# Diagonal 2-D prefix sum: the last 16 rows of the last batch loaded in batch 0 by ScalarE's DMA queue

## The chip, the cores and the metric

One core of one Trainium2 chip runs the kernel. The metric is the device time of one execution in microseconds (us). Before the change the median of three runs is 667.26 us (667.2 to 668.1).

## The reference

The input `x` is 4 batches of 4224 x 4224 fp32 numbers. The output is, per batch, the running sum along the diagonal of the two-dimensional prefix sum:

```python
ps = np.cumsum(np.cumsum(x, axis=1), axis=2)
diag = np.diagonal(ps, axis1=1, axis2=2)
return np.cumsum(diag, axis=1).astype(np.float32)
```

Every element of a batch is needed: element (i, j) enters all diagonal sums from max(i, j) on. So the kernel has to read 4 x 4224 x 4224 x 4 bytes, 285.5 MB, and to write 67.6 KB.

## The kernel before

**The main stream.** A batch is read in strips of 768 rows (`F2 * P`, six rows on each of 128 partitions) and one of 384 rows. GpSimd issues these loads (`load_rows`, L74 to L78), and the DMA turns fp32 into bf16 on the way. Three strip buffers are used in turn, so a load is issued as soon as the strip that lay in its buffer three strips earlier has been summed. Of a strip, `add_up` (L349 to L379) sums what lies left of the diagonal block by rows (ScalarE, `act_sum`, L258, and VectorE, `row_sums`, L267) and what lies right of it by columns (TensorE matmuls with a column of ones). The diagonal block is split by a triangular mask on VectorE. When a batch is through, matmuls put the row sums into groups, and two scans make the prefix sums.

**The last batch** is cut so that little work is left behind its last byte. Its last 384 rows do not come as one strip. A first piece, columns 3696 on of rows 3840 to 4095, was loaded at the very start by SyncE's queue as fp32 (`head`, L68). The rest of these 256 rows comes in two pieces (`part_a`, L451). The last 128 rows, columns 0 to 4095, come in four blocks of `R` = 32 rows (`part_b`, L462). A row of a block is cut in four pieces of 1024 columns, so that a block fills 128 partitions; its sums then go through `weights4`, a matrix that says how often the row on partition p counts for output i when four partitions hold one row. The last block is loaded in two DMAs, columns 0 to 767 of each piece and the other 256 (`bcut`, L453).

**The tail's order of work** is written out by hand (L528 to L581). Blocks 0 to 3 of `part_b` are summed as they come: block 0 by TensorE, block 1 and block 2 each in one ScalarE and one VectorE instruction (`act_sum`, `pair_sum`), block 3 in one ScalarE and two VectorE instructions (L571 to L573). An addition on VectorE (L557) stands between block 2 and block 3. Three matmuls (L579) bring the sums of block 3 into `fin_e`, VectorE copies that out (L580), and SyncE's queue stores the last 32 outputs (L581).

**Queues.** GpSimd's DMA queue (the page's q0, software_dynamic) carries all the bf16 loads in the order of issue. SyncE's (q1, hardware_dynamic) carries `head` and the outputs. ScalarE issues no DMA. The instructions of the engines are fetched through queues of their own (q8 and q14).

Of the kernel before, what the change touches and what calls it, by code (L numbers as in the profile page):

```python
# [8 lines left out]
FP32 = mybir.dt.float32  # L9
BF16 = mybir.dt.bfloat16  # L10
I32 = mybir.dt.int32
AX = mybir.AxisListType
ALU = mybir.AluOpType
# [4 lines left out]
def kernel(  # L18
# [14 lines left out]
    nc = tc.nc  # L33

    B, H, W = x.shape
    N = H
    P = 128
# [4 lines left out]
    LB = B - 1  # L42
    LG = NG - 1
    T0 = LG * GW
    TB = N - P
# [3 lines left out]
    consts = ctx.enter_context(tc.tile_pool(name="consts", bufs=1))  # L49
# [4 lines left out]
    last = ctx.enter_context(tc.tile_pool(name="last", bufs=1))  # L54
# [13 lines left out]
    head = last.tile([P, 2, HC], FP32, name="head")  # L68
    nc.sync.dma_start(out=head, in_=src_a[:, :, N - HC : N])

    def strip_tile():
        return strips.tile([P, F2, N], BF16, name="strip")

    def load_rows(o, b, r0):  # L74
        f = o.shape[1]
        nc.gpsimd.dma_start(  # L76
            out=o, in_=x[b, r0 : r0 + f * P, :].rearrange("(p f) w -> p f w", f=f)
        )  # L78
# [20 lines left out]
    def upper_mask(f):  # L99
# [22 lines left out]
        out=um1,  # L122
        in_=um1,
        compare_op=ALU.is_gt,
        fill=0.0,
        base=0,
        pattern=[[1, GW]],
        channel_multiplier=-1,
# [5 lines left out]
        out=ident,  # L134
        in_=ident,
        compare_op=ALU.is_equal,
        fill=0.0,
        base=0,
        pattern=[[-1, P]],
        channel_multiplier=1,  # L140
# [27 lines left out]
    def between_groups(name, turned):  # L168
# [27 lines left out]
        out=weights,  # L196
        in_=weights,
        compare_op=ALU.is_ge,
        fill=0.0,
        base=0,  # L200
        pattern=[[1, GW]],
        channel_multiplier=-1,
# [3 lines left out]
    R = P // 4  # L206
# [3 lines left out]
        out=steps, in_=steps, scalar=2, op=ALU.arith_shift_right  # L210
    )
    weights4 = consts.tile([P, P], FP32, name="weights4")
    nc.vector.tensor_scalar_max(out=weights4, in0=steps, scalar1=0.0)

    ident_h = consts.tile([P, P], BF16, name="ident_h")
    nc.vector.tensor_copy(out=ident_h, in_=ident)

    def matmul(o, lhsT, rhs, start=False):
        nc.tensor.matmul(  # L219
            o, lhsT=lhsT, rhs=rhs, start=start, stop=False, skip_group_check=True  # L220
        )
# [36 lines left out]
    def act_sum(acc, src, own=None):  # L258
        w = src.shape[-1]
        dump = own  # L260
        if dump is None:
            dump = dumpool.tile([P, 2176], BF16, name="dump")
        nc.scalar.activation(  # L263
            out=dump[:, :w], in_=src, func=ACT.Copy, accum_out=acc
        )

    def row_sums(acc, src):  # L267
        nc.vector.reduce_sum(out=acc, in_=src, axis=AX.X)  # L268
# [3 lines left out]
    def pair_sum(acc, src):  # L272

        w = src.shape[-1] // 2
        pair = last.tile([P, w], FP32, name=f"pair{len(pairs)}")
        pairs.append(pair)
        nc.vector.scalar_tensor_tensor(
            out=pair[:, :w],
            in0=src[:, :w],
            scalar=1.0,  # L280
            in1=src[:, w:],
            op0=ALU.mult,
            op1=ALU.add,
            accum_out=acc,
        )
# [32 lines left out]
        masked(hmu[:, h, :w], head[:, h, HC - w : HC], um1[:, :w], hu[:, h : h + 1])  # L318
    nc.vector.tensor_sub(out=asum[:, :, 0], in0=hs[:, 0:2], in1=hu[:, 0:2])

    whole_sums = last.tile([NG, LB, GW], FP32, name="whole_sums")
    last_sums = last.tile([NG, GW], FP32, name="last_sums")

    for b in range(B):
# [10 lines left out]
        def row_of(j):  # L335
            return (j + t0) % NG
# [12 lines left out]
        def add_up(strip, f, r0, acc, um, wp=0, ws=None, by_rows=False):  # L349


            nw = f * P // GW
            g = r0 // GW
            hi = r0 + f * P
            for j in range(g + nw + by_rows, NG):
                for q in range(f):
                    columns(j, 0, GW, strip[:, q, j * GW : (j + 1) * GW], q > 0)
            if ws is None:
                ws = scalar_cols(r0)
            mu = mup.tile([P, f, f * P], BF16, name=f"mu{f}")  # L360
            block = strip[:, :, r0:hi]
            nc.vector.tensor_mul(out=mu, in0=block, in1=um)  # L362
            nc.vector.tensor_sub(out=block, in0=block, in1=mu)  # L363
            if by_rows:
                rowed = mup.tile([P, GW], FP32, name="rowed")
                row_sums(
                    rowed,
                    strip[:, :, hi : hi + GW].rearrange("p q c -> p c q"),
                )
            for h in range(nw):  # L370
                for q in range(f):
                    columns(g + h, 0, GW, mu[:, q, h * GW : (h + 1) * GW], q > 0)
            if by_rows:
                k = row_of(g + nw)
                matmul(d, sel_f[:, NG - 1 - k : 2 * NG - 1 - k], rowed)
            for q in range(f):
                if ws > wp:
                    act_sum(acc[:, q, 0:1], strip[:, q, wp:ws])
            row_sums(acc[:, :, 1], strip[:, :, ws:hi])  # L379
# [12 lines left out]
        for s in range(ns):  # L392
            strip = prefetched.pop(0) if prefetched else None
            if strip is None:
                strip = strip_tile()
                load_rows(strip, b, s * F2 * P)
            add_up(
                strip, F2, s * F2 * P, acc6[:, s], um6, by_rows=whole and s > 0
            )
            if not whole and s == 0:  # L400
                diag_b = last.tile([P, P], BF16, name="diag_b")
                nc.gpsimd.dma_start(out=diag_b, in_=x[b, TB:N, TB:N])
            if not whole and s == 1:
                row_sums(hs[:, 2:3], diag_b)
                masked(hmu[:, 2, :P], diag_b, um1[:, :P], hu[:, 2:3])
                nc.vector.tensor_sub(out=dtot, in0=hs[:, 2:3], in1=hu[:, 2:3])
                for h in range(3):
                    columns(LG, h * P, GW, hmu[:, h, : GW - h * P], h > 0)
        a6 = acc6[:, :ns]
        sum_up(a6)  # L410
        for h in range(2):
            ps = slice(h * HP, (h + 1) * HP)
            k = row_of(h)
            nc.vector.tensor_copy(  # L414
                out=r6[ps, k : k + 2 * ns : 2, :], in_=a6[ps, :, :, 1]
# [27 lines left out]
        if not whole:  # L443

            strip = strip_tile()
            part_a = strip[:, 0:2]
            part_b = strip[:, 2, :TB].rearrange("p (s c) -> p s c", s=4)
            spare = strip[:, 3, :]
            acuts = [(1536, N - HC), (0, 1536)]
            for c0, c1 in acuts:  # L450
                nc.gpsimd.dma_start(out=part_a[:, :, c0:c1], in_=src_a[:, :, c0:c1])  # L451
            CB = TB // 4
            bcut = 768  # L453
            for sb, c0, c1 in (
                (0, 0, CB),
                (1, 0, CB),
                (2, 0, CB),
                (3, 0, bcut),
                (3, bcut, CB),
            ):  # L460
                r0 = TB + sb * R
                nc.gpsimd.dma_start(  # L462
                    out=part_b[:, sb, c0:c1],
                    in_=x[b, r0 : r0 + R, :TB].rearrange("r (k c) -> r k c", k=4)[
                        :, :, c0:c1
                    ],
                )

            fold_a = psum_s.tile([P, 2, 256], FP32, name="fold_a")
            c0, c1 = acuts[0]  # L470
            fcuts = [c0, c0 + 768, c0 + 2048, c1]
# [13 lines left out]
        c1 = mup.tile([NG, GW], FP32, name="c1")  # L485
# [10 lines left out]
        for i, (to, src) in enumerate(((c1, d), (c2, c1))):  # L496
            nc.vector.tensor_tensor_scan(  # L497
                out=to,
# [14 lines left out]
        fin_e = psum_s.tile([1, R], FP32, name="fin_e")  # L513
# [7 lines left out]
        def weigh_b(rows, w, r0=0, start=False):  # L521

            m = P - R - r0
            matmul(fin_b[:, r0:], rows, w[..., :m], start=start)
            matmul(fin_e, rows, w[..., m : m + R], start=start)


        c0, c1 = acuts[1]  # L528
# [5 lines left out]
        nc.scalar.copy(out=by, in_=by_ps)  # L534
        weigh_b(dtot, weights, start=True)
        weigh_b(ones_col[0:1], last_sums[0:1, M0:])


        row_sums(asum[:, :, 1], fold_a)
# [10 lines left out]
        esum = last.tile([P, 3], FP32, name="esum")  # L550
        act_sum(bsum[:, 0, 0:1], part_b[:, 1, :512], spare[:, :512])
        pair_sum(bsum[:, 0, 1:2], part_b[:, 1, 512:])
        for i in (1, 0):
# [5 lines left out]
            out=out[:LB, :].rearrange("b (g i) -> g b i", i=GW), in_=whole_sums  # L559
        )  # L560
        nc.sync.dma_start(
            out=out[b, :T0].rearrange("(g i) -> g i", i=GW), in_=last_sums[1:NG]
        )
        nc.sync.dma_start(
            out=out[b, T0 : T0 + M0].unsqueeze(0), in_=yl[:, :M0]
        )
        for i in (1, 0):
            weigh_b(bsum[:, 1, i : i + 1], weights4, 2 * R)


        act_sum(esum[:, 0:1], part_b[:, 3, :320], spare[:, 960:1280])  # L571
        pair_sum(esum[:, 1:2], part_b[:, 3, 320:bcut])
        pair_sum(esum[:, 2:3], part_b[:, 3, bcut:])  # L573
        nc.scalar.copy(out=yl[:, M0:E0], in_=fin_b)
        nc.sync.dma_start(
            out=out[b, T0 + M0 : T0 + E0].unsqueeze(0), in_=yl[:, M0:E0]
        )
        for k in (1, 0, 2):
            matmul(fin_e, esum[:, k : k + 1], weights4[:, :R])  # L579
        nc.vector.tensor_copy(out=ye, in_=fin_e)  # L580
        nc.sync.dma_start(out=out[b, T0 + E0 : N].unsqueeze(0), in_=ye)  # L581

# [29 lines left out]
```

## Time and profile before

| | |
|---|---|
| median of 3 runs | 667.26 us (667.2 to 668.1) |
| span of the profiled execution, first to last instruction | 665.7 us (the page gives no other time of it) |
| VectorE busy | 379.8 us (57%) |
| TensorE busy | 214.2 us (32%) |
| ScalarE busy | 135.3 us (20%) |
| GpSimd busy | 31.7 us (5%) |
| read from memory over the span | 285.47 MB, 429 GB/s |
| last data needed, seen by the waiting instruction | between 662.62 and 662.96 us |

The DMA lines of the page count the bytes as they are written, that is bf16 for the loads through GpSimd's queue: a packet of 25344 bytes there has read 50688. The share of an engine's busy time is a mean over stages; what holds the time is read from who waits for whom.

### The profile page before, as it was taken

To read this page: it belongs to the slowest core of one execution; us is meant where nothing else is said; L and a number is where in the kernel's file an instruction comes from. 1 tells how busy PE (TensorE), PEld (TensorE's weight loads), DVE (VectorE), ACT (ScalarE), POOL (GpSimd) and SP (SyncE) were. 2 spreads that over 40 slices of the span, in tenths; PEclk is the share of its full clock that TensorE was granted. 3 is DMA by queue.
4 is the path that set the end of the run, shared out by engine and by line. 5 is a ranking of instruction groups with operands and counts; after the bars stand their busy time and mean duration, and the time that the engine had idled before them with its cause. 6 is when DMAs were issued, how large, how long until landed. Compare 5 with 4: busy or idle time off the path is not lost.

```text
span 665.7 us, 2592 instructions
## 1 busy us (share of the span) xinstructions
PE 214.2 (32%) x998; PEld 98.5 (15%) x998; DVE 379.8 (57%) x176; ACT 135.3 (20%) x219; POOL 31.7 (5%) x60
## 2 busy tenths in 40 slices
PE   0070522302118143140311623403031253250468
PEld 0030211100003021010100311201000121120224
DVE  4160928476946173756793526466589443352766
ACT  0000121406300103040630020304063002030433
POOL 4200000000000000000000000000000000001000
PEclk9995856566558585765555958567555595765779
DMA  9999999999999999999999999999999999999998
GB/s 203 219 218 219 219 219 219 209 212 216 219 221 216 218 220 217 219 216 210 216 218 218 219 216 218 219 218 219 216 212 216 221 218 215 218 218 219 215 206 163
DMA packets 7667, 143.25 MB, mean 215 GB/s; under 512 B 698, under 2 KB 998, under 8 KB 2150
## 3 DMA queue, kind: packets, MB, share of 16 engines
q0 software_dynamic: 7312, 142.47, 99.9%
q1 hardware_dynamic: 342, 0.61, 0.3%
q8 instruction: 8, 0.13, 0.1%
q14 instruction: 5, 0.04, 0.0%
HBM read 285.47 MB, written 0.07 MB: 429 GB/s over the span
## 4 chain that ended last, share of the span: by engine, by line
DVE 51%; another core or an unknown queue 35%; DMA 12%; PE 1%; issue 1%; POOL 1%; DVEq 0%; POOLq 0%
DVE acc L268 27%; DMA strip<-in_x_dram 12%; DVE mu L362 7%; DVE strip L363 7%; DVE rowed L268 7%; PE d L219 1%; DVE c L497 0%; DVE whole_sums L497 0%; POOL strip L462 0%; DVE pu L268 0%; DVE whole_sums L288 0%; POOL strip L451 0%; DVE acc L387 0%; DVE rows L414 0%
## 5 line engine op out<-in xcount | busy, mean ns | idle before, releaser
L263 ACT ACTIVATE dump<-strip 128x416 bf16<-128x416 bf16 (+5 forms) x105 | 122.0, 1161 | 519.4 <-DMA strip<-in_x_dram 516.7
L362 DVE TENSOR_TENSOR mu<-strip,um 128x4608 bf16<-128x4608 bf16 (+1 forms) x24 | 52.4, 2183 | 256.9 <-DMA strip<-in_x_dram 256.7
L268 DVE TENSOR_REDUCE acc<-strip 128x6 f32<-128x4608 bf16 (+6 forms) x23 | 195.9, 8518 | 0.4
L226 PEld LDWEIGHTS <-sel 128*11 128x11 bf16 x643 | 66.7, 104 | 474.8 <-issue 445.4
L219 PE MATMUL d<-strip,sel 128*11 128x384 bf16 x90 | 37.3, 415 | 279.9 <-DMA strip<-in_x_dram 279.9
L226 PE MATMUL d<-strip,sel 128*11 128x384 bf16 x441 | 117.1, 409 | 13.8 <-DMA strip<-in_x_dram 13.8
L363 DVE TENSOR_TENSOR strip<-strip,mu 128x4608 bf16<-128x4608 bf16 (+1 forms) x24 | 52.4, 2183 | 1.0
L219 PE MATMUL d<-mu,sel 128*11 128x384 bf16 x43 | 16.0, 373 | 108.4 <-DVE mu L362 108.4
L268 DVE TENSOR_REDUCE rowed<-strip 128x384 f32<-128x2304 bf16 x12 | 48.9, 4076 | 0.0
L226 PE MATMUL d<-mu,sel 128*11 128x384 bf16 x200 | 45.7, 363 | 0.0
L76 POOL DMA_DIRECT2D strip<-in_x_dram x23 | 15.7, 683 | 537.2 <-DVE acc L268 291.8
L263 ACT ACTIVATION_READ_ACCUMULATOR dump<-strip 128x1 f32 x105 | 19.5, 186 | 0.0
L219 PE MATMUL d<-rowed,sel_f 128*11 128x384 f32 x24 | 11.7, 573 | 21.7 <-DVE rowed L268 21.7
L219 PEld LDWEIGHTS <-sel 128*11 128x11 bf16 x134 | 13.7, 102 | 24.8 <-issue 12.7
L219 PE MATMUL d<-ident,rows 128*11 128x128 f32 x24 | 5.2, 378 | 16.8 <-DVE rows L423 16.8
L219 PE MATMUL fold<-um,ident_h 128*128 128x512 bf16 x28 | 7.9, 454 | 0.0
L268 DVE TENSOR_REDUCE pu<-d 11x1 f32<-11x384 f32 x4 | 2.2, 546 | 6.2 <-PE d L219 6.2
L102 DVE MEMSET um<- 128x4608 bf16 (+1 forms) x2 | 4.9, 2458 | 1.1 <-issue 1.1
L103 POOL TENSOR_SCALAR_AFFINE_SELECT um<-um 128x4608 bf16<-128x4608 bf16 (+1 forms) x2 | 5.2, 2612 | 7.2 <-DVE um L102 7.2
L219 PEld LDWEIGHTS d<-rowed,sel_f 128*11 128x11 f32 x24 | 1.4, 92 | 26.4 <-DVE rowed L268 26.1
L219 PEld LDWEIGHTS d<-ident,rows 128*11 128x11 f32 x24 | 2.6, 118 | 18.5 <-DVE rows L423 11.7
L219 PE MATMUL d<-halves,rows 128*11 128x64 f32 x48 | 5.3, 289 | 0.0
(119 smaller groups left out, 75.0 us busy)
## 6 DMA issues: line engine op xcount, KB each, us to landing
strip<-in_x_dram POOLq DMA_DIRECT2D x18, 6336.0 KB, 72.7
strip<-in_x_dram POOLq DMA_DIRECT2D x7, 3168.0 KB, 55.7
strip<-in_x_dram POOLq DMA_DIRECT2D x1, 1080.0 KB, 49.9
strip<-in_x_dram POOLq DMA_DIRECT2D x1, 768.0 KB, 52.9
strip<-in_x_dram POOLq DMA_DIRECT2D x3, 256.0 KB, 54.1
head<-in_x_dram SPq DMA_DIRECT2D x1, 528.0 KB, 3.9
strip<-in_x_dram POOLq DMA_DIRECT2D x1, 192.0 KB, 43.2
strip<-in_x_dram POOLq DMA_DIRECT2D x1, 64.0 KB, 28.6
```

The costliest lines, as they stand in the source:

```text
L76: nc.gpsimd.dma_start(out=o, in_=x[b, r0 : r0 + f * P, :].rearrange("(p f) w -> p f w", f=f))
L102: nc.vector.memset(um, 1.0)
L103: nc.gpsimd.affine_select(out=um, in_=um, compare_op=ALU.is_gt, fill=0.0, base=0, pattern=[[-1, f], [1, f * P]], channel_multiplier=-f,)
L219: nc.tensor.matmul(o, lhsT=lhsT, rhs=rhs, start=start, stop=False, skip_group_check=True)
L226: te.add_instruction(mybir.InstMatmult(start_tensor_calc=False, stop_tensor_calc=False, tile_position=(0, 0), tile_size=(P, P if lhsT.shap ...
L263: nc.scalar.activation(out=dump[:, :w], in_=src, func=ACT.Copy, accum_out=acc)
L268: nc.vector.reduce_sum(out=acc, in_=src, axis=AX.X)
L362: nc.vector.tensor_mul(out=mu, in0=block, in1=um)
L363: nc.vector.tensor_sub(out=block, in0=block, in1=mu)
```

## The change

Rows 4208 to 4223 (the last 16) of the last batch, columns 0 to 4095, no longer come at the end. ScalarE issues their loads in batch 0, eight behind its sums of strip 1 and eight behind those of strip 2, one DMA for each row. A row is cut in eight pieces of 512 columns, which go as fp32 to eight partitions: eight descriptors of 2048 bytes in a DMA, 128 in all. They land in the space of `head`, which has been read by then. VectorE sums them in the last batch (one `row_sums` behind strip 1), and one more matmul in the tail brings the 16 sums into `fin_e` through a new matrix `weights8`.

The last block of `part_b` then has 16 rows instead of 32, each cut in eight pieces of 512 columns, and is again loaded in two DMAs, of 256 columns each. Its three sums have 128, 128 and 256 columns instead of 320, 448 and 256, and go through `weights8`, too.

```diff
+    E = P // 8
+    steps8 = consts.tile([P, R], I32, name="steps8")
+    nc.gpsimd.iota(steps8, pattern=[[8, R]], base=15, channel_multiplier=-1)
+    nc.vector.tensor_single_scalar(
+        out=steps8, in_=steps8, scalar=3, op=ALU.arith_shift_right
+    )
+    weights8 = consts.tile([P, R], FP32, name="weights8")
+    nc.vector.tensor_scalar_max(out=weights8, in0=steps8, scalar1=0.0)
...
+    CE = TB // 8
+    ends = head[:, 0, :CE]
+    end_sums = last.tile([P, 1], FP32, name="end_sums")
...
+            if b == 0 and s in (1, 2):
+
+                for r in range((s - 1) * E // 2, s * E // 2):
+                    nc.scalar.dma_start(
+                        out=ends[r * 8 : r * 8 + 8],
+                        in_=x[LB, N - E + r, :TB].rearrange("(k c) -> k c", k=8),
+                    )
...
             if not whole and s == 1:
+                row_sums(end_sums, ends)
                 row_sums(hs[:, 2:3], diag_b)
...
-            bcut = 768
-            for sb, c0, c1 in (
-                (0, 0, CB),
-                (1, 0, CB),
-                (2, 0, CB),
-                (3, 0, bcut),
-                (3, bcut, CB),
+            bcut = CE // 2
+            for sb, rows, c0, c1 in (
+                (0, R, 0, CB),
+                (1, R, 0, CB),
+                (2, R, 0, CB),
+                (3, E, 0, bcut),
+                (3, E, bcut, CE),
             ):
                 r0 = TB + sb * R
                 nc.gpsimd.dma_start(
                     out=part_b[:, sb, c0:c1],
-                    in_=x[b, r0 : r0 + R, :TB].rearrange("r (k c) -> r k c", k=4)[
-                        :, :, c0:c1
-                    ],
+                    in_=x[b, r0 : r0 + rows, :TB].rearrange(
+                        "r (k c) -> r k c", k=P // rows
+                    )[:, :, c0:c1],
                 )
...
         weigh_b(ones_col[0:1], last_sums[0:1, M0:])
+        matmul(fin_e[:, R - E :], end_sums, weights8[:, :E])
...
-        act_sum(esum[:, 0:1], part_b[:, 3, :320], spare[:, 960:1280])
-        pair_sum(esum[:, 1:2], part_b[:, 3, 320:bcut])
-        pair_sum(esum[:, 2:3], part_b[:, 3, bcut:])
+        act_sum(esum[:, 0:1], part_b[:, 3, : bcut // 2], spare[:, 960 : 960 + bcut // 2])
+        pair_sum(esum[:, 1:2], part_b[:, 3, bcut // 2 : bcut])
+        pair_sum(esum[:, 2:3], part_b[:, 3, bcut:CE])
...
         for k in (1, 0, 2):
-            matmul(fin_e, esum[:, k : k + 1], weights4[:, :R])
+            matmul(fin_e, esum[:, k : k + 1], weights8)
```

## The prediction

> **What bounds the kernel now.** I read the page's slices and DMA queues first, then the windows and the chain of waits at the end, then the timeline of the last microseconds.
>
> ```profile
> DMA  9999999999999999999999999999999999999998
> GB/s 203 219 218 219 219 219 219 209 212 216 219 221 216 218 220 217 219 216 210 216 218 218 219 216 218 219 218 219 216 212 216 221 218 215 218 218 219 215 206 163
> q0 software_dynamic: 7312, 142.47, 99.9%
> q1 hardware_dynamic: 342, 0.61, 0.3%
> ```
>
> The 16 DMA engines are busy in every slice. GpSimd's queue fills 99.9% of their time, while the busiest compute engine has 57%. So DMA time is the bound from start to end: a load moved elsewhere does not vanish, and only work behind the last byte, or time lost by some of the 16 DMA engines, can change the end.
>
> The windows show the end (columns: stretch, length, busy of PE, PEld, DVE, ACT, POOL, clock, DMA share, GB/s written):
>
> ```profile
> 660.00:661.00 1.00, 1.00 (x14) 0.69 (x12) 0.90 (x4) 0.71 (x2) 0.00 (x0) 1.00 1.14 204
> 661.00:661.50 0.50, 0.50 (x8) 0.36 (x5) 0.00 (x0) 0.19 (x2) 0.00 (x0) 1.00 0.98 169
> 661.50:662.00 0.50, 0.50 (x14) 0.50 (x12) 0.30 (x1) 0.30 (x1) 0.00 (x0) 1.00 0.72 119
> 662.00:662.40 0.40, 0.40 (x11) 0.26 (x7) 0.40 (x3) 0.36 (x2) 0.00 (x0) 1.00 0.70 119
> ```
>
> The share falls in steps from 661 on: the 16 engines do not finish together. The trace's single packet records (the page's third part is their sum) say by how much. Each engine closes its part of a DMA with a 4-byte packet. For the last DMA these lie at 661.04, 661.15, 661.17, 661.23, 661.33, 661.33, about 661.8 to 661.9 for one, 662.12, 662.12, 662.13, 662.27, 662.28, 662.34, 662.36, 662.39 and 662.63 us. The spread, 1.6 us, builds up slowly: an engine never idles, so whatever extra packet it takes (16 KB of instructions about 1.1 us, 8 KB about 0.32) stays as lateness to the end. A wait for a load ends with the latest of the 16.
>
> ```profile
> 661.70 0.46 DVE L277 SCALAR_TENSOR_TENSOR pair<-strip 128x288 f32<-128x288 bf16 x1 [0.76 <-DMA strip<-in_x_dram]
> 662.08 0.41 DVE L557 TENSOR_TENSOR yl<-fin_a,last_sums 1x256 f32<-1x256 f32 x1
> 662.62 0.39 DVE L277 SCALAR_TENSOR_TENSOR pair<-strip 128x224 f32<-128x224 bf16 x1
> 662.96 0.29 DVE L277 SCALAR_TENSOR_TENSOR pair<-strip 128x128 f32<-128x128 bf16 x1
> 663.08 0.47 PE fin_e L219 x6
> 663.57 0.18 DVE ye L580
> ```
>
> The first four lines are the timeline, the last two the chain. VectorE waits for block 2 (661.70) and then for block 3 (662.62), each about 0.35 us behind the last engine's closing packet (661.34, which is 662.28 less 0.94 worked out below, and 662.28). The last sum begins at 662.96, and from there to the span's end at 665.7 everything is one chain.
>
> **The change, part by part.**
>
> *Tail loads.* The packet records have 229 ns from one 1536-element packet to the next, 154 for 1024 elements, 115 for 768 and 41 for 256. Block 3 is 128 packets of 768 elements and 128 of 256, eight of each on an engine: 8 x 115 + 8 x 41 = 1248, with two closing packets some 1.27 us. Now it is 8 x 41 twice: 656, with closing packets 0.68. Saved: 0.59 us on each of the 16 engines.
>
> *The new loads in batch 0.* Which engines carry them? The page's q1 has 342 packets. `head` is 256 rows of data, the outputs 33 + 10 + 3 pieces: 302. The other 40 close a DMA, and 40 = 16 + 11 + 10 + 1 + 1 + 1: the store of 11 groups used 11 engines, that of 10 groups 10, `head` with 128 partitions 16. So a DMA on such a queue takes as many engines as its outer dimension has parts, up to 16. A new DMA has 8 parts: 8 engines, one descriptor each. The store of 11 groups also shows what extra work does. Before it (at 497 us) and after it (at 557 us) five engines' lateness against the other eleven had fallen by 195 ns. Of the ten engines in the 10-group store, four are late at the end (662.27 to 662.63), the very last among them.
>
> The Trainium skill, "DMA: Bandwidth & Descriptors", section "Why a DMA increments its semaphore by 16 and not by 1", states that these queues use the lowest-numbered engines that their part count gives. By it the 16 DMAs pile up on engines 0 to 7, sixteen descriptors each, and 8 to 15 get none. The count of 40 agrees with the number of engines; which ones they are no view names.
>
> The price: `head`'s 2112-byte fp32 packets follow one another at 82 ns, so 2048 bytes cost 80. A closing packet is 9 to 22 ns. Low: 16 x (76 + 9) = 1.36 us (76 is 2048 bytes at the 26.9 bytes per ns that the 25344-byte packets read in 1886 ns). High: no overlap, 16 x (86 + 22) = 1.73. The nearest row is the 11-group store: 195 ns for three 1536-byte packets and a closing one, 65 each all told; scaled to 2048 bytes that gives 80 + about 14. I take 16 x 94 = 1.50 us. Below nothing is excluded: these packets are extra on engines that have no gap.
>
> *Sum for the wait.* The latest engine is one of the ten of the 10-group store, and the eight loaded ones are most likely among these: 8 in 10 that it gets the 1.50. If not, the next two (0.23 us earlier) decide. So the wait for block 2 moves by +1.50 to about 663.20, and block 3 is complete at 663.20 + 0.68 = 663.88 instead of 662.96.
>
> *The work behind it.* From block 2's arrival VectorE has its sum (0.38 to the next instruction's start), the addition of L557 (0.41), then the two sums of block 3. The first, 64 pairs, I price from 128 pairs in 0.29 and 224 in 0.39 at 0.22, 0.18 to the next start. The last sum starts 0.38 + 0.41 + 0.18 + 0.04 (gaps) = 1.01 behind block 2, at 664.21, and not at the data's 663.88: L557 now stands in the way. Before it was 662.96 - 661.70 = 1.26 behind. So of the 0.59 saved only 0.25 comes through. ScalarE (0.48 of `act_sum` on block 2, 0.19 of read-out, then 0.3 + 0.19 for 128 columns) ends 1.2 behind block 2, before the last sum's 1.30. The last sum, three matmuls, copy and store are as before. Sum: 1.50 - 0.25 = **+1.25 us**; by the second engine, which I hold for the less likely, +1.0.
>
> *Covered edits.* ScalarE's 16 issues: SyncE's rows have 0.23 to 0.44 us each, so eight take 1.8 to 3.5 us. Queued behind them are the sums of the next strip, whose wait for data is 25.98 and 23.62 us:
>
> ```profile
> 95.35 0.92 ACT L263 ACTIVATE dump<-strip 128x864 bf16<-128x864 bf16 x1 [25.98 <-DMA strip<-in_x_dram]
> 125.22 1.27 ACT L263 ACTIVATE dump<-strip 128x1280 bf16<-128x1280 bf16 x1 [23.62 <-DMA strip<-in_x_dram]
> ```
>
> Without that cover GpSimd's refill would be issued 3.5 us later, and a refill lands 72.7 us behind its issue (page, sixth part), so the queue would still not run dry. `steps8` and `weights8` (0.24 on GpSimd, 0.5 on VectorE, by the rows of `steps`) lie at 22 us, where VectorE idles 11.91 us. The sum of `ends`, some 0.65 us by `fold_a`'s row of the same shape, lies ahead of a VectorE wait of 16.91 us at 572 us. Its wait for the 16 DMAs is over hundreds of us earlier. The matmul of `end_sums` (two passes, 0.2 us) stands behind `last_sums` and ahead of data that now come 1.5 us later. All are nothing; without their cover together about 1.6 us.
>
> **Rivals.**
>
> 1. *The extra load falls on engines with room, or is spread.* Against: the 40 closing packets; four of ten candidates are late. For: no view names the engines, and lateness comes partly from instruction fetches, which may fall elsewhere in the changed program. Were it spread over 16, each would get 0.75: 0.75 - 0.25 = +0.5, 667.75. Were all eight loaded engines early ones (lateness up to 0.3), they would end at 661.33 + 1.50 - 0.59 = 662.24, and an unloaded one would decide, at 662.34 - 0.59 = 661.75: the loaded ones at 662.24 are still last. Block 2 is then complete 0.2 later than now (662.24 is 0.39 before 662.63, less the 0.59 that block 3 no longer takes), the last sum starts 1.01 behind it at 662.91, and the gain is 0.05: 667.2. With no lateness left at all from the new loads, it is the 0.25 of above: 667.0. Chance for spread 0.13, for room 0.12.
>
> 2. *The other side: small packets between large ones cost more than in a row.* Each new descriptor must wait its turn between 25344-byte packets. At 525 us two starts of the store's packets with one large packet between them are 1940 ns apart where large packets alone follow at 1867: 73 ns for 1536 bytes, nearly as in a row, which speaks against. If switching cost more than 0.10 us for a descriptor and its closing, 16 x 0.10 - 0.25 passes 1.35 and the kernel is measurably slower. At 0.108 (no overlap) it is +1.5, 668.75; one further 8 KB fetch on the latest engine, since ScalarE's program grows, makes it +1.8, 669.1. Chance 0.27.
>
> 3. *The tail gain comes through whole*, 0.59, because the addition of L557 does not hold VectorE up and no load piles up. Then 666.7. A gain over 1.3 us has no source in the profile: 0.59 is all that leaves the stream. Chance 0.03, with what I overlook.
>
> **The numbers.** The profiled span, 665.7, is 1.56 us under the median, 667.26. I put the shift on the median: 667.26 + 1.25 = **668.5**. Forecast 0.45 (668.1 to 668.7), rival 2 0.27, rival 1 0.25, rival 3 0.03. The range is 667.0 to 669.1: it takes in the spread and most of the room, and the high bound of the price with one fetch. About 0.2%, 1.33 us, is what a measurement of this kernel tells from no change. The forecast lies just inside it: of its 0.45 I give 0.10 to beyond, with rival 2's 0.27 that makes slower 0.37; faster 0.03; within 0.60.
>
> **What would show it.** Right: the waits for block 2 and block 3 near 663.2 and later, the last sum straight behind the first on VectorE; q1 with 128 + 128 more packets (8 closing ones for each of 16 DMAs), q0 with 128 data packets of 768 elements fewer and as many more of 256; a gap between half of the engines' last closing packets and the rest that has grown by 1.5 us. Spread: 256 closing packets. Wrong: the wait for block 2 no later than now, or a stall of ScalarE or GpSimd in batch 0 that lets a slice of the DMA row fall.

## The result, and the profile after

The changed kernel takes 668.47 us in the median of 19 runs (668.13 to 669.2), the kernel before 667.54 in 19 runs beside it (667.02 to 668.1). The ratio is 1.0015 with a 95% interval of [1.0008, 1.0022]: about 1.0 us slower, between 0.5 and 1.5. The forecast was 1.25 us. That the median also meets the forecast 668.5 is partly luck: the kernel before ran 0.28 us longer here than in its three earlier runs, and the shift is 0.93 between the medians. The profiled execution has a span of 666.5 us, 0.8 more than before.

The DMA lines of the page after the change (queue, kind, packets, MB, share of 16 engines):

```profile
DMA  9999999999999999999999999999999999999997
q0 software_dynamic: 7312, 142.34, 99.7%
q1 hardware_dynamic: 342, 0.61, 0.3%
q10 hardware_dynamic: 256, 0.26, 0.1%
```

The stream still fills every slice, the last one a little less. ScalarE's queue is q10: 256 packets, 128 of data and 128 closing ones, so each of the 16 DMAs ran on 8 engines. (The prediction looked for these packets in q1; the page lists a queue of their own.) The share of q10, 0.1%, looks like nothing; but it is a mean over 16 engines and hides how the load is divided among them.

The windows of the changed kernel's end (stretch, length, busy of PE, PEld, DVE, ACT, POOL, clock, DMA share, GB/s), and behind them the last window of the kernel before:

```profile
661.50:662.00 0.50, 0.50 (x11) 0.37 (x9) 0.50 (x3) 0.37 (x1) 0.00 (x0) 1.00 0.69 114
662.00:662.40 0.40, 0.40 (x4) 0.24 (x3) 0.01 (x1) 0.35 (x2) 0.00 (x0) 1.00 0.31 49
662.40:662.80 0.40, 0.40 (x8) 0.37 (x7) 0.00 (x0) 0.00 (x0) 0.00 (x0) 1.00 0.30 41
662.80:663.20 0.40, 0.40 (x13) 0.40 (x10) 0.40 (x3) 0.40 (x1) 0.00 (x0) 1.00 0.39 72
```

```profile
662.40:662.80 0.40, 0.30 (x8) 0.14 (x4) 0.26 (x2) 0.18 (x1) 0.00 (x0) 1.00 0.07 10
```

Before, the share was 0.70 until 662.40 and then fell to 0.07. Now a third of the engines' time is used from 662.00 to 663.20: a few late engines still work while the others are done. The last closing packet of a load lies at 663.15 us, 0.52 later than before, although by the prediction's packet prices each engine has 0.59 less to do in the tail.

VectorE's timeline at the end:

```profile
662.80 0.46 DVE L286 SCALAR_TENSOR_TENSOR pair<-strip 128x288 f32<-128x288 bf16 x1 [0.80 <-DMA strip<-in_x_dram]
663.19 0.41 DVE L579 TENSOR_TENSOR yl<-fin_a,last_sums 1x256 f32<-1x256 f32 x1
663.52 0.20 DVE L286 SCALAR_TENSOR_TENSOR pair<-strip 128x64 f32<-128x64 bf16 x1
663.67 0.28 DVE L286 SCALAR_TENSOR_TENSOR pair<-strip 128x128 f32<-128x128 bf16 x1
664.26 0.18 DVE L602 COPY ye<-fin_e 1x32 f32<-1x32 f32 x1 [0.31 <-PE fin_e L228]
```

Block 2 arrives at 662.80 instead of 661.70. Block 3 is no longer waited for: the four instructions follow one another without a gap, and the last sum starts 0.87 us behind block 2's arrival (before: 1.26). So 1.10 later at block 2, 0.39 won back behind it, 0.71 later at the last sum.

### The profile page after: what moved, and what is told of

It is laid out like the page before. It is cut to its first block, busy times and chain, and to the rows that moved or that the text cites. A ratio compares the mean times of both kernels' runs of the same rounds, so it can differ in the third digit from the quotient of the medians.

```text
span 666.5 us, 2627 instructions
## 1 busy us (share of the span) xinstructions
PE 215.8 (32%) x1000; PEld 98.7 (15%) x1000; DVE 380.4 (57%) x179; ACT 135.2 (20%) x219; POOL 31.8 (5%) x61
## 4 chain that ended last, share of the span: by engine, by line
DVE 52%; another core or an unknown queue 36%; DMA 5%; PE 4%; issue 2%; DVEq 0%; POOL 0%; POOLq 0%
DVE acc L277 27%; DVE mu L375 8%; DVE strip L376 8%; DVE rowed L277 7%; DMA strip<-in_x_dram 5%; PE fold L228 1%; PE d L228 1%; PE fold L235 1%; DVE c L518 0%; DVE whole_sums L518 0%; PE fold_a L235 0%; DVE pu L277 0%; PE fin_b L228 0%; DVE whole_sums L297 0%
```

## The experiments

Three theories were set against each other. **Pile-up**: sixteen descriptors on each of the same eight DMA engines make these late, and they stay late to the end. **Tail**: the loads are free, and the changed tail costs the time. **Queue**: bytes in a second queue cost their share on all 16 engines, whichever carry them. All times are medians, and each ratio is to runs of the kernel before on the same chip. Most of these intervals reach about 0.6 us to each side, as much as some of the differences, so the traces have to bear a part of the argument.

**The loads alone.** The loads of the changed kernel, the tail of before:

```diff
+            if b == 0 and s in (1, 2):
+                for r in range((s - 1) * E // 2, s * E // 2):
+                    nc.scalar.dma_start(
+                        out=ends[r * 8 : r * 8 + 8],
+                        in_=x[LB, N - E + r, :TB].rearrange("(k c) -> k c", k=8),
+                    )
```

The sum of `ends` is added, too, but not used.

> The 16 new loads and the sum of what they bring are added to the kernel before, the tail is that of before (32 rows in the last block, so the new sum is not used). Pile-up theory (sixteen descriptors on each of eight DMA engines make these 1.5 us later to the end): 1.2 to 1.5 us over before. Tail theory (the loads are free, the changed tail costs the 0.9 us): no difference to before. Queue theory (the bytes in the second queue cost their share on all 16 engines, 0.65 us, wherever they run): 0.6 to 0.7 over before.

668.77 us against 667.48, ratio 1.0018 [1.0009, 1.0027]: 1.2 us slower. The loads cost time with nothing changed in the tail; the tail theory falls. Block 2 arrives in its timeline as late as in the changed kernel (662.80):

```profile
662.82 0.46 DVE L278 SCALAR_TENSOR_TENSOR pair<-strip 128x288 f32<-128x288 bf16 x1 [0.81 <-DMA strip<-in_x_dram]
```

**The tail alone.** The changed kernel without that loop, without `row_sums(end_sums, ends)` and without the matmul of `end_sums`. It leaves the 16 rows out of the result.

> The tail of the changed kernel without the new loads, their sum and their matmul: the 16 last rows (columns 0 to 4095) are left out of the sums. Pile-up and queue theories: the last sum starts about 0.87 us behind block 2 instead of 1.26, and block 2 comes as before: 0.3 to 0.4 us under before. Tail theory: 0.9 us over before.

666.85 us against 667.48, ratio 0.9992 [0.9983, 1.0001]. The median is 0.63 lower, the interval reaches from 1.1 less to no difference. The tail does not cost; at best it gains some tenths. The two halves, +1.29 and -0.63, add up to 0.66 of the 0.93 between the medians of the whole change, within what the intervals leave open.

**One DMA of 16 parts** in place of 16 DMAs of 8:

```diff
+            if b == 0 and s == 1:
+                nc.scalar.dma_start(
+                    out=ends,
+                    in_=x[LB, N - E :, :TB].rearrange("r (k c) -> r k c", k=8),
+                )
```

> The changed kernel with the same 128 descriptors in one DMA whose outer dimension has 16 parts (behind strip 1). Pile-up theory: 16 closing packets in that queue instead of 128, eight descriptors on each of 16 engines, 0.65 us each: 0.65 less 0.39 of the tail, 0.2 to 0.3 us over before, 0.6 under the changed kernel. Tail and queue theories: as the changed kernel, 0.9 over before.

667.62 us against 667.48, ratio 1.0006 [0.9997, 1.0015]. With the same bytes in the same queue the change now costs 0.14 in the median. Its queue line:

```profile
q10 hardware_dynamic: 144, 0.26, 0.1%
```

144 packets are 128 of data and 16 closing ones: 16 engines. The queue theory falls with it. Two things changed at once here, however, the engines and the number of DMAs, so the next run kept the number of packets.

**Spread, with as many closing packets**: 8 DMAs of 16 parts, each the same 512 columns of all 16 rows.

```diff
+                for k in range((s - 1) * 4, s * 4):
+                    nc.scalar.dma_start(
+                        out=ends[k:P:8],
+                        in_=x[LB, N - E :, k * CE : (k + 1) * CE],
+                    )
```

> The changed kernel with its 128 descriptors of 2048 bytes and 128 closing packets kept, but in 8 DMAs of 16 parts instead of 16 DMAs of 8 parts (one DMA takes the same 512 columns of all 16 rows), four behind strip 1 and four behind strip 2. Pile-up theory: 0.77 us on each of 16 engines instead of 1.54 on eight, so 0.1 to 0.4 over before, as the one DMA. Rival (what the one DMA saved was the number of DMAs and their closing packets): as the changed kernel, 0.9 to 1.0 over before.

667.66 us against 667.47, ratio 1.0007 [0.9997, 1.0016], as the one DMA.

```profile
q10 hardware_dynamic: 256, 0.26, 0.1%
```

The line is the changed kernel's to the digit: the same packets, bytes and share. What differs is the engines, and the number of DMAs, 8 for 16; but between one DMA and eight the time does not change. In the medians 0.7 of the 0.93 us are gone. The interval still overlaps that of the changed kernel, but 8 of its 11 runs lie below 668.13, the lowest of that kernel's 19. With the packet records below (1.50 us on each of eight engines there, 0.75 on each of 16 here) this is the run that carries the verdict.

**Each load twice**, the second time into `head[:, 1, :CE]`:

```diff
-                    nc.scalar.dma_start(out=ends[r * 8 : r * 8 + 8], ...
+                    for to in (ends, head[:, 1, :CE]):
+                        nc.scalar.dma_start(out=to[r * 8 : r * 8 + 8], ...
```

> The changed kernel with each of the 16 loads issued twice, the second time into space that is not read again. Pile-up theory: eight engines 1.5 us later once more, 2.3 to 2.5 us over before. Tail theory: as the changed kernel, 0.9 over before. Queue theory: 0.65 more than the changed kernel, 1.6 over before.

670.24 us against 667.48, ratio 1.0042 [1.0029, 1.0055]: 2.8 us slower, the pile-up theory's side and a little beyond. The excess has a possible cause that none of the three theories named. ScalarE's timeline, its own queue's issues among its sums:

```profile
68.73 32.11 ACTq L417 DMA_DIRECT2D head<-in_x_dram  x15
100.94 0.92 ACT L272 ACTIVATE dump<-strip 128x864 bf16<-128x864 bf16 x1 [32.25 <-DMA head<-in_x_dram]
...
108.22 50.16 ACTq L417 DMA_DIRECT2D head<-in_x_dram  x15
158.47 1.27 ACT L272 ACTIVATE dump<-strip 128x1280 bf16<-128x1280 bf16 x1 [51.28 <-DMA head<-in_x_dram]
```

With 16 issues behind a strip, the last of them come only as earlier ones complete, and ScalarE stands for 32 and 50 us. Its sums are late, and so is the refill of a strip buffer, on GpSimd's timeline:

```profile
167.10 0.70 POOL L76 DMA_DIRECT2D strip<-in_x_dram  x1 [52.32 <-ACT dump L272]
```

In the changed kernel this refill is issued at 146.70. At 168 to 170 us the stream thins out here: some large packets take 2.2 to 3.3 us instead of 1.89. The closing packets of the load that ends at about 200 us say which engines lost by it. Against the changed kernel the engines without new loads close about 1.4 us later, though they carry nothing of the second pile; the eight loaded ones close 1.7 later in the median, little more than the 1.5 of that pile. So the thinning mostly held up the engines that were early, and most of the 2.8 us is the two piles; the rest was not separated.

**The loads in batch 2** (`if b == 2 and s in (1, 2)`):

> The changed kernel with its 16 loads in batch 2 instead of batch 0. Pile-up theory (an engine that is late stays as late to the end): as the changed kernel, 0.8 to 1.1 over before. Rival (lateness is worked off on the way, or it costs something to carry): different from the changed kernel by 0.4 us or more.

668.54 us against 667.47, ratio 1.0018 [1.0009, 1.0026], as the changed kernel. 330 us later in the stream the loads cost the same: within the interval, lateness is neither worked off nor added to.

**One DMA, and the addition behind block 3.** The addition that stands between block 2 and block 3 on VectorE, with the store of its result, is moved behind the sums of block 3.

```diff
         pair_sum(esum[:, 2:3], part_b[:, 3, bcut:CE])
+        nc.vector.tensor_add(out=yl[:, :M0], in0=fin_a, in1=last_sums[0:1, :M0])
+        nc.sync.dma_start(
+            out=out[b, T0 : T0 + M0].unsqueeze(0), in_=yl[:, :M0]
+        )
```

> The one DMA of 16 parts, and the addition of the first 256 outputs with its store moved behind the sums of block 3. Addition theory (it holds VectorE up between block 2 and block 3): the last sum starts 0.7 behind block 2, when block 3 is complete, instead of 0.86: 0.1 to 0.2 us under the one DMA, so 0.0 to 0.1 over before. Rival (TensorE, which has no gap in the tail any more, holds the end): as the one DMA, 0.1 to 0.2 over before.

667.89 us against 667.47, ratio 1.0005 [0.9996, 1.0014]: no gain over the 667.62 of the one DMA. In its timeline the last sum starts 0.67 behind block 2, as the theory said:

```profile
662.37 0.46 DVE L286 SCALAR_TENSOR_TENSOR pair<-strip 128x288 f32<-128x288 bf16 x1 [0.83 <-DMA strip<-in_x_dram]
663.04 0.29 DVE L286 SCALAR_TENSOR_TENSOR pair<-strip 128x128 f32<-128x128 bf16 x1
```

But look at SyncE's queue, and below it at the last store of the changed kernel:

```profile
663.69 0.23 SPq L591 DMA_DIRECT2D out_dram<-yl  x1
663.70 0.18 DVE L600 COPY ye<-fin_e 1x32 f32<-1x32 f32 x1
663.96 0.25 SPq L595 DMA_DIRECT2D out_dram<-yl  x1
664.26 0.25 SPq L601 DMA_DIRECT2D out_dram<-ye  x1
```

```profile
664.47 0.23 SPq L603 DMA_DIRECT2D out_dram<-ye  x1
```

The moved store and the one behind it now stand ahead of the last. It is issued 0.38 behind the end of its copy (663.88); in the changed kernel it was 0.03 (664.44 and 664.47). The copy itself starts 0.66 behind the last sum instead of 0.59, straight behind the moved addition. In this timeline, what the addition gave up, the queue of stores and this wait took.

**The same move in the kernel before**, as a control:

> The kernel before with the addition of the first 256 outputs and its store moved behind the sums of block 3. Store theory (moved back, the two stores of the first outputs stand ahead of the last store on SyncE's queue): the last store is issued 0.3 to 0.4 us behind its copy instead of 0.03, so 0.2 to 0.4 us over before. Rival (the order of stores is hidden): as before.

667.74 us against 667.33, ratio 1.0006 [0.9997, 1.0015]. In the timeline the copy starts at 663.25 and lasts 0.18, and the last store is issued at 663.86, 0.43 later:

```profile
663.25 0.18 DVE L580 COPY ye<-fin_e 1x32 f32<-1x32 f32 x1
663.29 0.23 SPq L571 DMA_DIRECT2D out_dram<-yl  x1
663.56 0.25 SPq L575 DMA_DIRECT2D out_dram<-yl  x1
663.86 0.25 SPq L581 DMA_DIRECT2D out_dram<-ye  x1
```

The median is 0.41 higher, as the store theory has it; the interval does not exclude no difference, so the timeline shows the wait, and its worth in time is likely, not settled.

**The rows through GpSimd's own queue**, as bf16, first with the late addition and then without it:

```diff
-    ends = head[:, 0, :CE]
+    ends = head[:, 0, : CE // 2].bitcast(BF16)
...
+                nc.gpsimd.dma_start(
+                    out=ends,
+                    in_=x[LB, N - E :, :TB].rearrange("r (k c) -> r k c", k=8),
+                )
```

> As the run with one DMA and the late addition, but the 16 rows come as bf16 through GpSimd's own queue, behind strip 1 of batch 0. Pile-up theory: eight packets of 512 elements on each engine, about 0.62 to 0.65 us against the 0.59 that block 3 saves, so as before within 0.2 us, and a little under the run with ScalarE's queue. Rival (a DMA in the second queue costs more than its packets): 0.4 us or more under the run with ScalarE's queue.

667.91 us against 667.47, ratio 1.0006 [0.9997, 1.0015]: the same as 667.89 through ScalarE's queue. The second queue shows no cost of its own. The 0.44 over before is more than the expected 0.2; the next run takes the late addition out.

> The 16 rows as bf16 through GpSimd's own queue behind strip 1 of batch 0, with the addition where the changed kernel has it. Store theory: 0.2 to 0.4 us under the run with GpSimd's queue and the late addition, so within 0.2 us of before. Rival (the addition's place makes no difference): as that run, 0.4 over before.

667.51 us against 667.33, ratio 1.0006 [0.9997, 1.0015]: 0.18 over in the median, within the noise of before. It is 0.4 under the run with the late addition, but the runs of before beside that one were 0.14 higher, and the two ratios are the same: what the late addition costs is again likely, not settled. Of all versions that read every row, none beats the kernel before.

## Why the prediction was right, point by point

**The bound.** DMA time from end to end: right. Moved bytes did not vanish; spread evenly they cost each engine 0.73 us where the tail saves 0.59.

**Eight engines.** Right: 128 closing packets for 16 DMAs. The prediction read it from 40 closing packets of other shapes. The Trainium skill, "DMA: Bandwidth & Descriptors", section "Why a DMA increments its semaphore by 16 and not by 1", states that the number of engines is the largest up to 16 that divides the outer dimensions, and that queues like SyncE's and ScalarE's take the lowest-numbered ones. The trace agrees with the number, 8; the engines' numbers are in no view. That all 16 DMAs took the same eight shows in the packet records: at the end of batch 0's loads, eight engines are 1.35 to 1.76 us behind the earliest, one is 1.07 behind (an instruction fetch), and seven lie within 0.27. The later store of 11 groups fits in: the five engines whose lateness falls by 0.19 to 0.20 us at it, those that it leaves out, are all among the eight without new loads.

**The price, 1.50 us on each.** Right. From the first strip's closing packets to those of batch 0's last load an engine without disturbance needs 134.53 us. The 16 together took 1.35 us more than that before and 13.70 after. Less the 1.35 and less an 8 KB instruction fetch (0.32) that fell into this stretch, 12.03 are left, 1.50 for each of eight. With one DMA of 16 parts it is 12.99 - 1.35 = 11.64, 0.73 for each of 16; spread over 8 DMAs 13.64 - 1.35 - 0.32 = 11.97, 0.75. The run with one DMA and the late addition is an exception: the same working gives about 0.9 for each engine, and 48 of its large packets took 1.90 to 2.10 us in this stretch instead of 1.89, 2.6 us more in all, which is most of the excess. In the other three the total hardly changes. What counts is the latest engine.

**The saving behind block 2, 0.25.** 0.39: the addition's start and the next sum's are 0.33 apart, not 0.41, and the small sum takes 0.15 to the next start instead of 0.18, with no gaps. The order was right: VectorE ran through, and block 3 was not waited for.

**The wait for block 2, +1.50.** The mis-sized term: it moved by 1.10 between the two profiles. The prediction put the whole load on the very engine that was last before, and let the lateness of 1.6 us build up slowly. But that engine had started 1.29 us late, as its closing packet of the first strip shows, and no engine of the changed kernel's profile was then more than 0.40 behind. This start differs from one execution to the next (0.50 to 1.99 us at that point in the other profiles), so the latest engine's lateness is partly drawn anew each time. The loads add in full to eight engines, but to the maximum of all 16 only as far as one of the eight leads it. So this is part of what the prediction's rival of engines with room described. Each profile is one execution; in the medians the loads alone cost 1.2 to 1.3 us.

**Covered edits.** Right: ScalarE's issues took 0.28 to 0.58 us each, and the next strips' sums still waited 26.70 and 24.24 us for data; the sum of `ends` (0.68 us) ran ahead of a wait of 16.35 us. The sentence that even without this cover the stream could not run dry was not tested for the 3.5 us that it priced. With each load twice the refill came 20.4 us later (167.10 instead of 146.70), and the stream did thin out.

**Rivals.** The spread rival was priced at +0.5 and was made: +0.14 to +0.19 in the medians. The rival of dearer switching between queues did not occur; 1.50 for sixteen is 0.094 each, below the 0.10 from which it would have decided. The tail gain did not come through whole: 0.39 of 0.59.

## What to carry to other kernels

Where DMA time is the bound, as here, a load that is moved out of the tail is not saved. What matters is the latest of the 16 DMA engines: look at how many engines each small DMA takes, since here 16 narrow ones put all their time on the same eight and that lateness lasted to the end. One DMA whose outer dimension has 16 parts carried the same bytes at half the price for the latest engine.

A tail written out by hand has an order on each queue, the store queue included. Moving an addition behind the critical sum also moved its store close ahead of the critical store; the timelines show that store waiting 0.4 us, and no gain was left.

## What the runs showed of the hardware that was not expected

A small DMA beside a full stream is cheap in engine time and slow to finish. In the changed kernel the packets of a new DMA start 3.8 us after those of the one ahead of it, about two large packets of 1.89 us: in the packet records one large packet lies between the data packet and the closing packet, and one more before the next DMA's data. Eight DMAs needed 29 us (71.2 to 100.0), more than the strip's own wait that was to cover them. Eight issues did not hold ScalarE up; sixteen did, for 32 and 50 us. How many the queue takes before it holds the issuing engine was not measured.
